# Pinning the issue order of operand splits and of pair sums, and merging the stores of hidden tiles, in a hybrid decoder step

## The chip, the cores and the metric

The kernel runs on one core of one Trainium2 chip. The metric is the device time of one execution in microseconds (us); before the change it is 2970.54 us, the median of three runs (2969.29 to 2973.55). The core has five engines that are named here as in the profile: PE (matmuls; PEld is its weight loads), DVE (vector engine), ACT (scalar engine), POOL (GpSimd) and SP, which does no arithmetic and issues all of this kernel's loads and stores.

## The reference

One layer of a decoder trunk on 1024 prompt tokens and 64 sample tokens, all in fp32. A first half-step SwiGLU feed-forward network, a token mixing with two branches (windowed pooling and a state-space scan), a second half-step SwiGLU network, and a final norm:

```python
def swiglu(x, w_in, w_out):
    gu = x @ w_in
    g, u = gu[..., :D_FF], gu[..., D_FF:]
    return (jax.nn.silu(g) * u) @ w_out
...
    x = x + 0.5 * swiglu(rmsnorm(x, norm_ffn1[l]), ffn1_w_in[l], ffn1_w_out[l])
    mix, new_pool, new_conv, new_ssm = token_mixing(
...
    x = x + mix
    x = x + 0.5 * swiglu(rmsnorm(x, norm_ffn2[l]), ffn2_w_in[l], ffn2_w_out[l])
```

D_MODEL is 1024 and D_FF is 2816, so the hidden layer has 22 blocks of 128 rows. The change touches the hand-over of the hidden layer `silu(g) * u` to the product with `w_out`, in both networks.

## The kernel before

**Numbers.** Each fp32 operand is split into a high part in the PE's 32-bit matmul format and the remainder; a product is then three matmuls (high with high, low with high, high with low). A split is two instructions: ACT copies the operand into the high part (`hh`, `hp`, `wh`), DVE subtracts that from the operand for the low part (`hr`, `hp`, `wl`). `split` (L357 for ACT, L359 for DVE) does it for tiles of activations, and `parts` (L759, L760) for weights. `parts` runs at high priority, `split` doesn't.

**Halves.** The 1088 tokens are worked in two halves of 512 and 576 tokens (h = 0, 1). FFN1's and FFN2's first matmul (`ffn_in`) runs over the 22 hidden blocks `ff` and, for each, over the halves. The result of one block and half is a tile `g`, whose two parts (slices `f` and `s_`, 256 or 288 columns each) are the two column halves of a Strassen-Winograd scheme.

**`hidden` and `hidden_odd`.** Two consecutive blocks `ff` make a pair: the even one is kept as `e`, the odd one arrives as `g`. The second matmul is done as seven products "1" to "7", each of which needs its own operand made of these four quarters: "1" is `e[f]`, "2" and "3" are `g[f]` and `g[s_]`, and "5", "6", "7" and "4" are results of four subtractions on POOL (L708), each in place over a quarter that is no longer needed. Every operand is stored to device memory into a tile `hb<product>_<pair>` (L691 for "1", L699 for the others) as soon as it exists: seven stores for each pair and half. The subtractions are a chain that starts `H_AT` = 0.3 us after `hidden_odd`, one step per `H_PACE` = 0.3 us, by the modelled PE time below.

**`second`.** The second matmul runs through the products in the order "1256473". A product has four units m (128 output columns each). A unit reads eleven X tiles (k = 0 to 10, one per pair) in three chunks of weights, kb = 0, 4 and 8, and runs 66 matmuls into two PSUM tiles `po`, one per half. `weights` gives a chunk: raw weights `wraw` are loaded (L748), for products 5, 6, 7 and 3 POOL adds or subtracts them (`ws`, L777 to L792), and `parts` makes `wh` and `wl` from it. `fetch_X` (L726 to L738) loads the X tiles of a product (`hr`, or `hp` where the tile is one of a ring of eight pairs) from `hb`; after each unit it issues up to three loads of the next product. `split_X` (L740 to L743) splits what has been loaded. It is called at the start of a product and, in `unit`, just before the chunk kb = 8. `leave` (L824) takes a finished `po` into the sums, and `old` (L794) adds old results that are loaded as `xo` (L798, L804).

**What sets the order.** The program is traced in the order in which the generators run. `tick` runs the chains (`start`, `later`) whose due time, counted in modelled PE time `pe[0]`, has come. A scheduler then orders the traced instructions on each engine by priority and by when its own model says that operands are ready, so an instruction can stand on its engine ahead of others that were traced before it. `keep_in_program_order` ties an instruction behind the one that was traced before it on the same engine. All engines work in order: what stands behind a waiting instruction waits too. SP issues loads and stores of all stages in one order.

**FFN1's loads.** While the first matmul of FFN1 runs, the second half's x is loaded in pieces `xin` (L965) and transposed on PE (`ptr`, helper L170; other matmuls come from the helper L166: `pu`, `pg` and `pw` are `ffn_in`'s PSUM tiles). Weight parts for later are stored and loaded in between (`part`, `pr`, L311 to L318).

Of the kernel before, what the change touches and what calls it, by code (L numbers as in the profile page):

```python
# [8 lines left out]
F32 = mybir.dt.float32  # L9
F32R = mybir.dt.float32r  # L10
I32 = mybir.dt.int32
AF = mybir.ActivationFunctionType
ALU = mybir.AluOpType

P = 128
# [27 lines left out]

N_FP = 4
NK2, N2, HALF_AT = NFF // 2, 544, (0, 256)
H_AT, H_PACE = 0.3, 0.3
AHEAD = {'2': 11, '5': 11, '6': 8, '4': 8, '7': 10, '3': 10}
STEP = (5.0, 3.8)
STEP_S = 1.0
# [15 lines left out]
def tile_hybrid_pool_ssd_macaron(  # L65
# [10 lines left out]
    V, S, T, G = nc.vector, nc.scalar, nc.tensor, nc.gpsimd  # L76
    dma = nc.sync.dma_start
# [3 lines left out]
    dp = ctx.enter_context(tc.tile_pool(name="dram", bufs=1, space=bass.MemoryType.DRAM))  # L81
# [7 lines left out]
    def act(shape=(P, 576), dt=F32, name="a"):  # L89
        return sp.tile(list(shape), dt, tag="act", bufs=N_ACT, name=nm(name))  # L90

    def pair(n, name="hl"):
        t = sp.tile([P, 2, 576], F32R, tag="pair", bufs=N_PAIR, name=nm(name))
        return t[:, 0, :n], t[:, 1, :n], t
# [16 lines left out]
    def fx(dt=F32, name="x"):  # L111
        if stage["name"] == "mix":
            return act((P, 576), dt, name)
        return stage["p"].tile([P, 592], dt, tag="fx", bufs=N_FX, name=nm(name))
# [22 lines left out]
    def start(gen, delay=0.0):  # L137
        c = Chain(gen, delay)
        chains.append(c)
        return c  # L140
# [214 lines left out]
    def split(src, hi, lo, scale=1.0):  # L355

        S.activation(hi, src, AF.Identity, scale=scale)  # L357
        if isinstance(scale, float) and scale == 1.0:
            V.tensor_tensor(lo, src, hi.bitcast(F32), op=ALU.subtract)  # L359
        else:  # L360
            V.scalar_tensor_tensor(lo, src, scale, hi.bitcast(F32), op0=ALU.mult, op1=ALU.subtract)
# [253 lines left out]
    def ffn_in_plain(wi, ff, x):  # L615

        h = x[0]
        g = fx(name="g")
        pg, pu = banks([x], "pd", "pg")[0], banks([x], "pd", "pu")[0]
        for kb in (0, 4):  # L620
            ws = [load_w(wi, kb, 4, c0 + ff * P) for c0 in (0, FF)]
            for kk in range(4):
                for pts, (wh, wl) in zip((pg, pu), ws):
                    products([pts], wh, wl, kk, slice(0, P), [x], kb + kk, KD)
                    tick()
        func(g, pg, h, AF.Silu)
        for pt, (a, b) in zip(pu, PIECES[h]):
            V.tensor_tensor(g[:, a:b], g[:, a:b], pt[:, : b - a], op=ALU.mult)
        hidden(h, ff, g)
# [46 lines left out]
        yield from gen  # L676


    hblock = {p: [dp.tile([P, N2], F32, tag=f"hb{p}_{i}", name=f"hb{p}_{i}") for i in range(NK2)] for p in "1234567"}
    even, hsums = [None, None], []  # L680

    def hidden(h, ff, g):

        if ff == NFF - 1:
            hlast.append(lambda: hidden_odd(h, ff, g))
        elif ff % 2:
            hidden_odd(h, ff, g)
        else:
            even[h] = g
            n, at = NPAIR[h], HALF_AT[h]  # L690
            dma(hblock["1"][ff // 2][:, at : at + n], g[:, :n])  # L691

    def hidden_odd(h, ff, g):

        n, i, at = NPAIR[h], ff // 2, HALF_AT[h]
        f, s_ = slice(0, n), slice(n, 2 * n)

        def put(p, x):
            dma(hblock[p][i][:, at : at + n], x)  # L699

        e = even[h]
        put("2", g[:, f])
        put("3", g[:, s_])

        def sums():
            for p, out, a, b in (("5", e[:, s_], e[:, s_], e[:, f]), ("6", g[:, s_], g[:, s_], e[:, s_]),
                                 ("7", e[:, f], g[:, s_], e[:, f]), ("4", g[:, f], g[:, f], g[:, s_])):
                G.tensor_tensor(out, a, b, op=ALU.subtract)  # L708
                put(p, out)
                yield H_PACE  # L710

        hsums.append(start(sums(), H_AT))

# [2 lines left out]
    def second(wo, after, half):  # L716
# [9 lines left out]
        def fetch_X(p, n):  # L726
            for k in range(len(X[p]), min(len(X[p]) + n, NK2)):
                if k >= 4:
                    a, r = act((P, 576), F32R, "hh"), act((P, 576), name="hr")
                elif p == "1":  # L730
                    a, r = fx(F32R, "hh"), fx(name="hr")
                else:
                    a, r, _ = pair(576, "hp")
                    r = r.bitcast(F32)
                a, r = a[:, :N2], r[:, :N2]
                dma(r, hblock[p][k])  # L736
                raws.append((k, r, a))
                X[p].append((a, r.bitcast(F32R)))  # L738

        def split_X(below=NK2):  # L740
            while raws and raws[0][0] < below:
                _, r, a = raws.pop(0)
                split(r, a, r.bitcast(F32R))  # L743

        def raw(par, mh, m, kb, nk):
            t = sp.tile([P, 4 * P], F32, tag="wraw", bufs=N_RAW, name=nm("wraw"))[:, : nk * P]
# [77 lines left out]
        def leave(p, m, h, pt):  # L824
# [30 lines left out]
            else:  # L855
                add(a[:, s_], a[:, s_])

        fetch_X("1", NK2)
        split_X()
        while hlast:  # L860
            hlast.pop(0)()
        while hsums:
            finish(hsums.pop(0))
        for p, nxt in zip(order[:-1], order[1:]):
            split_X(8)
            fetch_X(p, NK2)
            for m in range(4):
# [10 lines left out]
                n = AHEAD[nxt] - len(X[nxt])  # L878
# [1089 lines left out]
```

## Time and profile before

| | |
|---|---|
| median of three runs | 2970.54 us |
| profiled execution, its own time | 2973.63 us |
| its span, first to last instruction | 2971.9 us |
| PE busy | 2805.6 us (94%) |
| DVE, ACT, POOL busy | 62%, 47%, 46% |
| mean granted PE clock | 0.978 |
| DMA, of 16 engines' span | 54.9% |
| stores of hidden tiles | 308 issues |
| ACT splits of X tiles | 154 (106 `hh`, 48 `hp`) |

A row of the table of waits names the waiting engine, its PSUM or SBUF tile and line, then the releaser: the engine or transfer whose end came last before the wait ended. A row of a timeline gives the start in us from the span's start, the length, the engine and line, the operation with its tiles (out<-in, buffer numbers left out), how many in a row, and in square brackets the idle time before it and the releaser. The granted clock is the share of full speed that the PE was given; a matmul at half clock takes almost twice as long and counts as busy.

The stages that concern the change lie as follows: FFN1's first matmul up to 561 us, FFN1's `second` from 561 to about 840 us, FFN2's first matmul up to about 2686 us, FFN2's `second` from there to the end.

### The profile page before, as it was taken

What the parts mean: (1) busy time and instruction counts of PE and PEld (TensorE: products, weight loads), DVE (VectorE), ACT (ScalarE), POOL (GpSimd) and SP (SyncE); (2) the same over time, 40 slices, a digit from 0 to 9 for tenths busy, and PEclk for the clock granted to TensorE, in tenths of its full rate; (3) what the DMA queues carried; (4) which work ended last, traced back from release to release, by engine and by line L of the source; (5) the groups of instructions that cost most, each with busy time, mean ns of one, the idle gap of its engine ahead of it and who ended that gap; (6) DMA issues with size and microseconds to landing.
All of it is one profiled execution on the core that took longest, in us unless ns stands there. A gap on an engine that the chain in (4) does not pass through costs nothing. (4 is left out here: it accounts for less than half of the span.)

```text
span 2971.9 us, 54814 instructions
## 1 busy us (share of the span) xinstructions
PE 2805.6 (94%) x19834; PEld 2622.8 (88%) x19834; DVE 1852.5 (62%) x2848; ACT 1396.8 (47%) x3086; POOL 1354.8 (46%) x1424
## 2 busy tenths in 40 slices
PE   7989999989999999999999999898999999999888
PEld 6888899888979999999987887677999999989887
DVE  6645555656685486867676767866665554556665
ACT  5444444533354465555545656566233444444333
POOL 5645665344452264655632233323135656561651
PEclk9999999999999999999999999998999999999999
DMA  4566543576635555554367577786774333336772
GB/s 134 157 214 194 177 135 99 185 219 193 208 109 153 161 168 179 167 162 131 99 207 222 181 221 243 239 258 186 228 253 145 100 103 103 98 121 197 229 234 85
DMA packets 566864, 512.50 MB, mean 172 GB/s; under 512 B 39860, under 2 KB 435496, under 8 KB 566584
## 3 DMA queue, kind: packets, MB, share of 16 engines
q1 hardware_dynamic: 566576, 508.99, 54.9%
q8 instruction: 156, 2.56, 0.4%
q14 instruction: 116, 0.95, 0.1%
q10 hardware_dynamic: 16, 0.00, 0.0%
HBM read 361.28 MB, written 147.80 MB: 171 GB/s over the span
## 5 line engine op out<-in xcount | busy, mean ns | idle before, releaser
L166 PE MATMUL pw<-X,wh 128*128 128x288 f32 (+2 forms) x2832 | 634.6, 312 | 11.5 <-ACT v L566 9.8
L166 PEld LDWEIGHTS pw<-X,wh 128*128 128x128 f32 x2832 | 466.8, 191 | 35.7 <-ACT v L566 11.1
L166 PE MATMUL pw<-X,wl 128*128 128x288 f32 (+1 forms) x1644 | 476.8, 290 | 0.9 <-DVE wl L450 0.9
L450 DVE TENSOR_TENSOR wl<-s,wh 128x512 fp32r<-128x512 f32 x288 | 249.1, 866 | 285.4 <-ACT wh L449 263.9
L166 PE MATMUL pw<-hl,wh 128*128 128x256 f32 (+1 forms) x1536 | 392.0, 328 | 3.4 <-DVE t L570 3.3
L166 PE MATMUL pw<-hi,wh 128*128 128x288 f32 x1120 | 331.3, 296 | 2.4 <-ACT t L602 1.4
L166 PE MATMUL pw<-hi,wl 128*128 128x288 f32 x1120 | 330.0, 295 | 0.0
L166 PE MATMUL pw<-lo,wh 128*128 128x288 f32 x1120 | 329.7, 294 | 0.0
L443 POOL TENSOR_TENSOR s<-wraw,wraw 128x512 f32<-128x512 f32 x144 | 196.3, 1363 | 280.7 <-DVE wl L450 205.2
L166 PEld LDWEIGHTS pw<-X,wl 128*128 128x128 f32 x1644 | 315.1, 192 | 1.1 <-DVE wl L450 1.1
L166 PE MATMUL pw<-hl,wl 128*128 128x256 f32 x1072 | 300.3, 280 | 0.0
L166 PEld LDWEIGHTS pw<-hl,wh 128*128 128x128 f32 x1536 | 258.9, 189 | 24.5 <-DVE t L570 3.7
L449 ACT ACTIVATE wh<-s 128x512 fp32r<-128x512 f32 x288 | 181.0, 629 | 155.0 <-PE pw L166 129.7
L450 DVE TENSOR_TENSOR wl<-wraw,wh 128x512 fp32r<-128x512 f32 x216 | 177.5, 822 | 115.7 <-ACT wh L449 106.7
L166 PE MATMUL po<-hh,wh 128*128 128x256 f32 (+1 forms) x848 | 191.6, 298 | 31.6 <-ACT wh L759 31.5
L166 PEld LDWEIGHTS pw<-hi,wh 128*128 128x128 f32 x1120 | 210.5, 188 | 9.6 <-ACT t L602 2.0
L166 PEld LDWEIGHTS pw<-lo,wh 128*128 128x128 f32 x1120 | 210.6, 188 | 0.0
L166 PEld LDWEIGHTS pw<-hi,wl 128*128 128x128 f32 x1120 | 210.1, 188 | 0.2
L166 PEld LDWEIGHTS pw<-hl,wl 128*128 128x128 f32 x1072 | 203.0, 189 | 0.0
L449 ACT ACTIVATE wh<-wraw 128x512 fp32r<-128x512 f32 x216 | 135.5, 627 | 138.6 <-PE pw L166 117.3
L166 PE MATMUL po<-hh,wl 128*128 128x256 f32 (+1 forms) x848 | 191.0, 297 | 3.0 <-DVE wl L760 2.8
L166 PE MATMUL po<-hr,wh 128*128 128x256 f32 (+1 forms) x848 | 189.8, 295 | 1.0 <-DVE hr L359 1.0
(397 smaller groups left out, 6817.7 us busy)
## 6 DMA issues: line engine op xcount, KB each, us to landing
wraw<-in_ffn_w_in_dram SPq DMA_DIRECT2D x188, 256.0 KB
wraw<-in_ffn_w_out_dram SPq DMA_DIRECT2D x144, 256.0 KB
wraw<-in_w_in_dram SPq DMA_DIRECT2D x144, 256.0 KB
wh<-part SPq DMA_DIRECT2D x116, 256.0 KB
wl<-part SPq DMA_DIRECT2D x116, 256.0 KB
hr<-hb SPq DMA_DIRECT2D x106, 272.0 KB
hb<-g SPq DMA_DIRECT2D x154, 144.0 KB
hb<-g SPq DMA_DIRECT2D x154, 128.0 KB
```

The lines of the kernel that those rows point to most:

```text
L166: T.matmul(out, lhsT, rhs, start=start, stop=stop, skip_group_check=free)
L443: G.tensor_tensor(t, a, b, op=op)
L449: S.activation(wh, a, AF.Copy)
L450: V.tensor_tensor(wl, a, wh.bitcast(F32), op=ALU.subtract)
```

## The change

**Stores.** The seven tiles `hb` of a pair become four: "1" alone, and "23", "75" and "46" as tiles that hold two products side by side. "2" and "3" are stored in one transfer of both quarters of `g`. The four subtractions run without stores between them, 0.5 us apart, starting 3.0 us after `hidden_odd`; 3.0 us after the last, "75" (the tile `e`) and "46" (the tile `g`) are stored in one transfer each. So a pair and half has four stores in place of seven, of the same bytes. Loads remain one per product and pair.

**Order of the subtractions.** They and the two late stores are pinned to the traced order on their engines. For the first pair of each network (ff = 1) they run on DVE, otherwise on POOL.

**Splits of X tiles.** The ACT half of `split_X` is pinned to the traced order (and is the function Copy in place of Identity); the DVE half is not pinned.

On ACT, at the end of a unit of a product whose weights are sums (FFN1's `second`); `wh` are weight chunks, `hp` and `hh` the high parts of X tiles. Before:

```order
665 L759 ACTIVATE wh_8646<-ws_8640 128x512
666 L357 ACTIVATE hp_8748<-hp_8748 128x544
667 L357 ACTIVATE hp_8750<-hp_8750 128x544
668 L357 ACTIVATE hp_8752<-hp_8752 128x544
669 L759 ACTIVATE wh_8680<-ws_8674 128x512
670 L759 ACTIVATE wh_8714<-ws_8708 128x384
671 L357 ACTIVATE hp_8872<-hp_8872 128x544
672 L357 ACTIVATE hh_8874<-hr_8875 128x544
673 L357 ACTIVATE hh_8877<-hr_8878 128x544
```

The first chunk of a unit is followed by three splits of tiles of the next product, then the unit's other two chunks. Now:

```order
663 L767 ACTIVATE wh_8547<-ws_8541 128x512
664 L767 ACTIVATE wh_8581<-ws_8575 128x512
665 L767 ACTIVATE wh_8615<-ws_8609 128x384
666 L750 ACTIVATE hh_8527<-hr_8528 128x544
667 L750 ACTIVATE hh_8530<-hr_8531 128x544
668 L767 ACTIVATE wh_8669<-ws_8663 128x512
669 L767 ACTIVATE wh_8703<-ws_8697 128x512
670 L767 ACTIVATE wh_8737<-ws_8731 128x384
671 L750 ACTIVATE hp_8649<-hp_8649 128x544
672 L750 ACTIVATE hp_8651<-hp_8651 128x544
673 L750 ACTIVATE hp_8653<-hp_8653 128x544
```

The same three splits (`hp`, last three rows) stand behind the unit's third chunk (384 columns) and behind all three chunks of the unit after it; two splits of the product before stand where they stood.

On ACT, at the passage from FFN1's first matmul to `second`; L602 and L607 are `ffn_in`'s last evacuations, `wh<-wraw` chunks of product 1. Before:

```order
538 L602 COPY t_6268<-pw_1102_6315 128x288
539 L357 ACTIVATE hh_6386<-hr_6387 128x544
540 L357 ACTIVATE hh_6389<-hr_6390 128x544
541 L759 ACTIVATE wh_6465<-wraw_6463 128x512
542 L357 ACTIVATE hh_6392<-hr_6393 128x544
543 L357 ACTIVATE hh_6395<-hr_6396 128x544
544 L759 ACTIVATE wh_6495<-wraw_6493 128x512
545 L357 ACTIVATE hp_6554<-hp_6554 128x544
546 L607 ACTIVATE g_6269<-g_6269 128x288
547 L759 ACTIVATE wh_6525<-wraw_6523 128x384
548 L357 ACTIVATE hp_6651<-hp_6651 128x544
```

Seven `hh` splits of product 1 stand further up, between the weight chunks of the first matmul, and the last four of it here, among the first three chunks. Now (the row of L602 and the first two `hh` are the three rows ahead of these):

```order
532 L767 ACTIVATE wh_6366<-wraw_6364 128x512
533 L750 ACTIVATE hh_6299<-hr_6300 128x544
534 L750 ACTIVATE hh_6302<-hr_6303 128x544
535 L750 ACTIVATE hh_6305<-hr_6306 128x544
536 L750 ACTIVATE hh_6308<-hr_6309 128x544
537 L607 ACTIVATE g_6176<-g_6176 128x288
538 L750 ACTIVATE hh_6311<-hr_6312 128x544
539 L750 ACTIVATE hh_6314<-hr_6315 128x544
540 L750 ACTIVATE hh_6317<-hr_6318 128x544
541 L750 ACTIVATE hh_6320<-hr_6321 128x544
542 L750 ACTIVATE hh_6323<-hr_6324 128x544
543 L767 ACTIVATE wh_6396<-wraw_6394 128x512
```

All eleven splits of product 1 stand behind L602, five of them between L607 and the second chunk. On DVE the low parts follow them in the same way, seven `hr` between its last work for `ffn_in` (L609) and the `wl` of that second chunk.

On SP, in FFN1's first matmul; `hb` are the stores of hidden tiles, `xin` the pieces of x, `part` and `pr` prepared weights, `wraw` weights. Before:

```order
108 L699 DMA hb2_1_278<-g_259_1540 128x256
109 L469 DMA wraw_413_2369<-in_ffn1_w_in_dram 128x4x128
110 L699 DMA hb2_1_278<-g_264_1558 128x288
111 L699 DMA hb6_1_322<-g_259_1540 128x256
112 L699 DMA hb7_1_333<-g_146_866 128x256
113 L699 DMA hb6_1_322<-g_264_1558 128x288
114 L699 DMA hb4_1_300<-g_259_1540 128x256
115 L699 DMA hb7_1_333<-g_230_1373 128x288
116 L699 DMA hb4_1_300<-g_264_1558 128x288
117 L317 DMA part_317_1853<-ph_315_1850 128x512
118 L318 DMA part_319_1854<-pr_300_1768 128x512
119 L965 DMA xin2_323_1873<-in_x_prompt_dram 128x512
```

The load of `xin2_323` follows the stores of products "2", "6", "7" and "4" of a pair, each of the last three behind its subtraction. Now:

```order
98 L705 DMA hb23_1_278<-g_259_1499 256x1x256
99 L705 DMA hb23_1_278<-g_264_1519 256x1x288
100 L317 DMA part_317_1800<-ph_315_1797 128x512
101 L318 DMA part_319_1801<-pr_300_1728 128x512
102 L973 DMA xin2_323_1821<-in_x_prompt_dram 128x512
103 L311 DMA pr_329_1859<-in_ffn2_w_in_dram 128x4x128
104 L705 DMA hb75_1_289<-g_146_832 256x1x256
105 L705 DMA hb46_1_300<-g_259_1499 256x1x256
106 L973 DMA xin2_335_1914<-in_x_prompt_dram 128x512
```

That load stands behind the "23" stores alone; of the pair's late stores the first two come after it.

```diff
@@ -43,7 +43,7 @@
 
 N_FP = 4
 NK2, N2, HALF_AT = NFF // 2, 544, (0, 256)
-H_AT, H_PACE = 0.3, 0.3
+H_AT, H_PACE, H_OUT = 3.0, 0.5, 3.0
 AHEAD = {'2': 11, '5': 11, '6': 8, '4': 8, '7': 10, '3': 10}
 STEP = (5.0, 3.8)
 STEP_S = 1.0
@@ -676,7 +676,13 @@
         yield from gen
 
 
-    hblock = {p: [dp.tile([P, N2], F32, tag=f"hb{p}_{i}", name=f"hb{p}_{i}") for i in range(NK2)] for p in "1234567"}
+    hblock = {}
+    for ps_ in ("1", "23", "75", "46"):
+        for i in range(NK2):
+            t = dp.tile([P, len(ps_), N2], F32, tag=f"hb{ps_}_{i}", name=f"hb{ps_}_{i}")
+            hblock[ps_, i] = t
+            for j, p in enumerate(ps_):
+                hblock[p, i] = t[:, j, :]
     even, hsums = [None, None], []
 
     def hidden(h, ff, g):
@@ -688,26 +694,27 @@
         else:
             even[h] = g
             n, at = NPAIR[h], HALF_AT[h]
-            dma(hblock["1"][ff // 2][:, at : at + n], g[:, :n])
+            dma(hblock["1", ff // 2][:, at : at + n], g[:, :n])
 
     def hidden_odd(h, ff, g):
 
         n, i, at = NPAIR[h], ff // 2, HALF_AT[h]
         f, s_ = slice(0, n), slice(n, 2 * n)
 
-        def put(p, x):
-            dma(hblock[p][i][:, at : at + n], x)
+        def put(ps_, x):
+            return dma(hblock[ps_, i][:, :, at : at + n], x[:, : 2 * n].rearrange("p (a t) -> p a t", a=2))
 
         e = even[h]
-        put("2", g[:, f])
-        put("3", g[:, s_])
+        put("23", g)
 
         def sums():
-            for p, out, a, b in (("5", e[:, s_], e[:, s_], e[:, f]), ("6", g[:, s_], g[:, s_], e[:, s_]),
-                                 ("7", e[:, f], g[:, s_], e[:, f]), ("4", g[:, f], g[:, f], g[:, s_])):
-                G.tensor_tensor(out, a, b, op=ALU.subtract)
-                put(p, out)
+            for out, a, b in ((e[:, s_], e[:, s_], e[:, f]), (g[:, s_], g[:, s_], e[:, s_]),
+                              (e[:, f], g[:, s_], e[:, f]), (g[:, f], g[:, f], g[:, s_])):
+                tc.keep_in_program_order((V if ff == 1 else G).tensor_tensor(out, a, b, op=ALU.subtract))
                 yield H_PACE
+            yield H_OUT
+            for ps_, x in (("75", e), ("46", g)):
+                tc.keep_in_program_order(put(ps_, x))
 
         hsums.append(start(sums(), H_AT))
 
@@ -733,14 +740,15 @@
                     a, r, _ = pair(576, "hp")
                     r = r.bitcast(F32)
                 a, r = a[:, :N2], r[:, :N2]
-                dma(r, hblock[p][k])
+                dma(r, hblock[p, k])
                 raws.append((k, r, a))
                 X[p].append((a, r.bitcast(F32R)))
 
         def split_X(below=NK2):
             while raws and raws[0][0] < below:
                 _, r, a = raws.pop(0)
-                split(r, a, r.bitcast(F32R))
+                tc.keep_in_program_order(S.activation(a, r, AF.Copy))
+                V.tensor_tensor(r.bitcast(F32R), r, a.bitcast(F32), op=ALU.subtract)
 
         def raw(par, mh, m, kb, nk):
             t = sp.tile([P, 4 * P], F32, tag="wraw", bufs=N_RAW, name=nm("wraw"))[:, : nk * P]
```

## The prediction, made before the changed kernel was run

> **What bounds the kernel now.** I read the page first, then PE's busy time by stage, then what PE waited for, then the engine named there, then single stalls in order of time.
>
> ```profile
> span 2971.9 us, 54814 instructions
> PE 2805.6 (94%) x19834; PEld 2622.8 (88%) x19834; DVE 1852.5 (62%) x2848; ACT 1396.8 (47%) x3086; POOL 1354.8 (46%) x1424
> ```
>
> PE is the bound: 166.3 us of the span are all that earlier issue can recover, besides time at a low clock. The table by stretch says where that lies. Its columns are the stretch and its length, busy time of PE, PEld, DVE, ACT and POOL (with instruction counts), granted clock, DMA share, GB/s.
>
> ```profile
> 70.00:130.00 60.00, 52.83 (x360) 50.35 (x359) 39.12 (x53) 23.31 (x55) 36.82 (x33) 0.94 0.46 140
> 130.00:300.00 170.00, 156.21 (x1007) 145.97 (x1006) 88.56 (x156) 73.04 (x171) 84.42 (x85) 0.94 0.64 205
> 560.00:640.00 80.00, 74.41 (x571) 72.66 (x571) 42.56 (x68) 34.18 (x66) 13.00 (x11) 0.98 0.67 201
> 640.00:760.00 120.00, 103.66 (x786) 101.63 (x786) 71.21 (x98) 37.70 (x66) 67.65 (x54) 0.96 0.73 213
> 760.00:780.00 20.00, 19.42 (x133) 19.10 (x133) 17.86 (x24) 8.61 (x15) 17.87 (x15) 0.83 1.11 321
> 2690.00:2880.00 190.00, 172.39 (x1317) 169.62 (x1316) 108.05 (x153) 65.86 (x119) 76.75 (x61) 0.96 0.71 213
> 2880.00:2900.00 20.00, 17.98 (x126) 17.66 (x127) 18.19 (x25) 8.16 (x15) 16.68 (x14) 0.83 1.10 313
> ```
>
> 70 to 300 us is FFN1's first matmul (idle 7.2 and 13.8 us). 560 to 780 and 2690 to 2900 us are the two passes of `second` (idle 22.5 and 19.6 us). All of them show clocks under 1. What ended PE's idle time, over the whole span (total, times, longest):
>
> ```profile
> PE po L166 <- ACT wh L759: 33.8, 11, 7.2
> PE ptr L170 <- DMA xin<-in_x_sample_dram: 8.1, 2, 4.4
> PE po L166 <- DVE wl L760: 6.9, 9, 1.3
> PE ptr L170 <- DMA xin<-in_x_prompt_dram: 5.7, 2, 5.2
> PE pu L166 <- ACT wh L296: 4.9, 1, 4.9
> ```
>
> `po` belongs to `second`, `ptr` and `pu` to FFN1. ACT, which releases `po`, was itself waiting; first two rows 555 to 835 us, last two 2680 to 2972 us:
>
> ```profile
> ACT hp L357 <- DMA hp<-hb: 39.8, 12, 8.7
> ACT hh L357 <- DMA hr<-hb: 39.4, 16, 6.6
> ACT hp L357 <- DMA hp<-hb: 39.7, 13, 8.3
> ACT hh L357 <- DMA hr<-hb: 33.9, 17, 5.1
> ```
>
> One stall in order of time (start, length, engine, line, count):
>
> ```profile
> 749.58 1.29 POOL L786 TENSOR_TENSOR ws<-wraw,wraw 128x512 f32<-128x512 f32 x1 [1.62 <-DMA wraw<-in_ffn_w_out_dram]
> 751.87 1.44 SPq L736 DMA_DIRECT2D hp<-hb  x3
> 752.62 0.41 PE L166 MATMUL po<-hp,wh 128*128 128x256 f32 x2
> 752.87 0.41 PE L166 MATMUL po<-hp,wl 128*128 128x256 f32 x2
> 756.58 2.16 ACT L357 ACTIVATE hp<-hp 128x544 fp32r<-128x544 f32 x3 [7.96 <-DMA hp<-hb]
> 758.65 1.03 ACT L759 ACTIVATE wh<-ws 128x512 fp32r<-128x512 f32 x2
> 759.32 0.82 PE L166 MATMUL po<-hh,wh 128*128 128x256 f32 x2 [6.04 <-ACT wh L759]
> ```
>
> The sum `ws` was ready at 750.9. Its cast `wh` (758.65) stood on ACT behind three splits of X tiles whose loads were issued only at 751.87. PE had nothing left from 753.3 and started 0.67 us after that cast. The X tiles split there are read in the next product, after this cast's matmuls; their splits had been let ahead of a cast that was urgent.
>
> **The change, part by part.**
>
> *Splits pinned behind the casts traced before them.* The order now has a unit's three casts, then two or three splits. Counted in the orders on SP and PE, the next cast behind a split is first read 73 to 110 matmuls after the point at which that split's load can be issued at the old stall sites, and at least 127 now, mostly 180 to 480 for `hp`. At 0.125 us a matmul (the two PE rows of two above start 0.25 us apart) 73 are 9.1 us, which the ACT waits of up to 8.7 us plus the splits (0.7 us each) use up; 127 are 15.9 us, which they don't. So I take the `wh` waits as gone: −33.8 us. The `wl` waits stay (6.9): the DVE half isn't pinned.
>
> Stalls cost twice, since a low clock follows. After the shortest of the longer ones:
>
> ```profile
> 2705.53 0.70 PE L166 MATMUL po<-hh,wh 128*128 128x256 f32 x2 [2.35 <-ACT wh L759]
> 2708.35 0.66 PE L166 MATMUL po<-hh,wh 128*128 128x256 f32 x2
> ```
>
> Six pairs of matmuls lie between these starts, without idle time: 2.82 / 6 = 0.47 us a pair where 0.25 is usual. The shortfall of the clock in the table, (1 − clock) × length, is 1.6 + 4.8 + 3.4 = 9.8 us in the first pass and 7.6 + 3.4 = 11.0 in the second; part of it lies inside the idle time, so I take 8 each: −16. The Trainium skill (TensorE: Matmul & The Clock Gate, Part 1) says that the clock halves after an idle window of about 3.4 us. The trace disagrees for this stall: 2.35 us of idle were enough. By the page such a stall would cost no dip; with three of them below its figure, at some 1.3 us each (2.82 − 6 × 0.25), the term would be −12 by an estimate.
>
> *New block at the start of each pass.* All eleven splits of product 1 now stand behind FFN-in's last ACT work, five of them and seven DVE halves between L607/L609 and the second cast.
>
> ```profile
> 556.14 0.38 ACT L602 COPY t<-pw 128x288 f32<-128x288 f32 x1
> 560.90 0.41 PE L166 MATMUL po<-hh,wh 128*128 128x256 f32 x2
> 562.89 0.44 DVE L609 TENSOR_TENSOR g<-g,pw 128x288 f32<-128x288 f32 x1
> L357 ACT ACTIVATE hh<-hr x11: 642/649/667, 544.1 to 561.0; 128x544 fp32r<-128x544 f32 x11
> L359 DVE TENSOR_TENSOR hr<-hr,hh x11: 711/915/1291, 546.0 to 563.3; 128x544 fp32r<-128x544 f32 x11
> ```
>
> Before, the eleven were done from 544 on, beside FFN-in's matmuls. Now ACT starts them at 556.5. DVE's L609 may end up to one split (0.65) earlier than at 563.3, since no split stands ahead of the activation it reads; from 562.7, seven halves at 0.65 to 1.2 us (rows overlap by some 0.07) and one `wl` of 0.7 end between 568.0 and 571.8. The order puts the matmul that reads this `wl` 32 matmuls into the pass, 564.9 by 560.90 + 32 × 0.125. The stall is 3.1 to 6.9 us; by the median (0.915) 4.4, and a clock dip of 2 to 3 us follows. I take +7 for each pass (ends 2 and 10): +14.
>
> *FFN1: sums without stores between, three stores instead of six.*
>
> ```profile
> 145.28 7.41 SPq L699 DMA_DIRECT2D hb<-g  x7
> 153.71 0.45 SPq L965 DMA_DIRECT2D xin<-in_x_prompt_dram  x1
> 157.95 1.11 PE L170 MATMUL ptr<-ident,xin 128*128 128x128 f32 x4 [5.20 <-DMA xin<-in_x_prompt_dram]
>   DMA hb<-g: 38.4, 27
> ```
>
> SP spent 7.4 us on seven stores that waited, one by one, for GpSimd's sums (the last row: GpSimd idle before those sums until a store had landed); the load of `xin` behind them came 5.2 us late. In the new order this load stands ahead of the pair's "75" and "46" stores, and so do those behind the two later stalls (the 8.1 us row). −13.8 us of waits; of the clock's 0.06 × 170 = 10.2 us I take −8. A later `xin` moves the other way, from 85 matmuls of lead to 54, behind four stores: +4 (ends 0 and 6). Net −17.8.
>
> *First pair's sums on VectorE.*
>
> ```profile
> 73.70 1.55 POOL L708 TENSOR_TENSOR g<-g,g 128x256 f32<-128x256 f32 x2 [7.89 <-DVE g L628]
> 85.51 0.85 PE L166 MATMUL pu<-hi,wh 128*128 128x288 f32 x2 [4.93 <-ACT wh L296]
> ```
>
> GpSimd stood 7.89 us with the X chain of the second half queued behind a sum; that chain then held ACT, whose cast released PE at 85.51. Freed of it, some 6 of the stage's 7.2 us of idle go (4.9 here and part of the rest, which follows it), and 2.5 of the clock's 0.06 × 60 = 3.6. Against this, DVE's second sum must wait for the "23" store to land with a weight split behind it: +1.5 to 5, I take 3.5. Net −5. The 16 sums themselves, half as wide as an `hr` split (0.7 to 1.3), are under 1 us each on an engine busy for 39 of 60 us there.
>
> *Nothing.* Bytes are unchanged. Copy in place of Identity changes 154 splits of 0.65 us on an engine that is busy 47%; even 0.1 us more each would be hidden by its idle time, and without that idle time cost 15. 132 issues fewer on SP cost nothing where SP isn't waited for; the later stores of "75" and "46" are read two products on. From 300 to 540 and in FFN2's first matmul PE is full, so there is no gain there.
>
> Sum: −33.8 − 16 + 14 − 17.8 − 5 = −58.6 us. The profiled execution took 2973.6 (span 2971.9 plus 1.7), 3.1 above the median of 2970.5; 2970.5 − 58.6 = 2912.
>
> **Rivals.**
>
> *A: the transfers are the limit behind the splits.* Product 7 needs per unit two sets of raw weights, a quarter of eleven X tiles and a tile of `xo`:
>
> ```profile
> wraw<-in_ffn_w_out_dram SPq DMA_DIRECT2D x144, 256.0 KB
> hp<-hb SPq DMA_DIRECT2D x48, 272.0 KB
> ```
>
> 2 × (256 + 256 + 192) + 748 + 272 KB = 2.49 MB in 66 × 0.125 = 8.25 us, or 301 GB/s. The table shows 321 and 313 once each, for it, but 213 over 120 and 190 us, against. At 213 a unit takes 11.7 us: +3.4 × 4 × 2 = +27, 2939. The Trainium skill (DMA: Bandwidth & Descriptors, Specifications) gives about 358 GB/s of HBM per core, by which this rival costs nothing.
>
> *B: slower. The pinned splits become the wait.* A split that waits for its load now always holds the next unit's casts and the drains of PSUM on ACT. Now 40.7 us of PE idle (33.8 + 6.9) stand against 152.8 us of ACT waits for X loads (the four rows), 27%. If a share s came through, the change would be (152.8 s − 40.7) × 1.39 (the dips, 16 on 40.7) + 14 − 22.8. That is zero at s = 0.31 and +41 (3011) at 0.5. For it: nothing else may pass a waiting split. Against: the leads counted above.
>
> *C: the block at the start is hidden*, since loads or L609 come earlier: −58.6 − 14, 2898.
>
> *D: FFN1 gains nothing*, because the loads there are held by another store, and passes gain little beyond the block: within 6 us of 2970.
>
> **How the numbers follow.** Forecast 0.53, A 0.2, B 0.12, C 0.1, D 0.05. 0.2% is 6 us, about what a measurement can tell from no change. Faster: forecast, A and C, 0.83; the same 0.05; slower 0.12. The range reaches from C with the wider ends of the FFN1 terms (2885) past A to 2958, where A meets a block of 10 us in each pass and a smaller clock gain; it leaves out B and D.
>
> **What would show it.** Right: no `wh` stall over 2 us in either pass, granted clock 0.98 or more from 600 to 760, the waits of ACT for `hp` still there but no longer PE's; a stall of 3 to 7 us within 40 matmuls of a pass's first; no `ptr` stall at the second to fourth `xin`. Wrong: `po` waits on `wh` behind a split in most units (B), POOL's sums or `wraw` as releasers with DMA near 1 over product 7 (A), or a new wait of SP for a sum ahead of `xin` (D).

## The result, and the profile after

The changed kernel takes 2935.06 us (median of four, 2933.76 to 2937.11), the kernel before 2972.05 us in the same comparison: a ratio of 0.9866 (95% interval 0.9833 to 0.9900). By the medians it is faster by 37 us (1.2%), where 58.6 were forecast (the medians alone give 0.9876; the four runs of the kernel before include one of 2986.93 us). The profiled execution took 2934.26 us.

The page of the kernel after, its span and engines:

```profile
span 2932.5 us, 54478 instructions
PE 2793.1 (95%) x19834; PEld 2614.3 (89%) x19834; DVE 1876.5 (64%) x2864; ACT 1399.6 (48%) x3086; POOL 1349.2 (46%) x1408
```

The same matmuls run on PE in nearly the same order in both kernels, so their start times can be compared one by one. The table takes the same matmul (by its number on PE) in the two profiled executions. The last column is the forecast for that stretch.

| matmul, at us before | what lies there | after minus before, us | since the row above | forecast |
|---|---|---|---|---|
| 40.0 | ahead of anything the change touches | +3.2 | +3.2 | 0 |
| 103.2 | first pair's sums done | −0.2 | −3.4 | −5 |
| 551.8 | end of FFN1's first matmul | −17.3 | −17.1 | −17.8 |
| 572.3 | 11 us into the first pass of `second` | −8.9 | +8.4 | +7 |
| 802.6 | end of that pass | −28.7 | −19.8 | −24.9 |
| 2668.6 | end of FFN2's first matmul | −31.4 | −2.7 | 0 |
| 2694.1 | 8 us into the second pass | −21.4 | +10.0 | +7 |
| 2958.3 | last matmul | −39.0 | −17.6 | −24.9 |

(At the first of these matmuls the traces of all versions stand between −0.2 and +3.2 us, although the change touches nothing ahead of it; this part isn't the change's.)

PE's busy time by stretch, after (columns as before):

```profile
70.00:130.00 60.00, 54.45 (x368) 51.51 (x367) 43.78 (x69) 23.77 (x57) 25.45 (x23) 0.97 0.50 149
130.00:300.00 170.00, 164.36 (x1104) 153.05 (x1104) 101.04 (x164) 77.55 (x184) 100.54 (x97) 1.00 0.70 222
540.00:560.00 20.00, 12.16 (x74) 11.26 (x73) 15.55 (x18) 9.02 (x17) 10.07 (x9) 0.83 0.66 217
560.00:640.00 80.00, 80.00 (x642) 80.00 (x641) 45.63 (x68) 35.14 (x66) 14.68 (x11) 1.00 0.66 192
640.00:720.00 80.00, 78.43 (x628) 78.21 (x626) 64.25 (x80) 29.65 (x51) 54.45 (x43) 1.00 0.79 235
720.00:760.00 40.00, 33.31 (x231) 32.21 (x232) 27.11 (x36) 15.48 (x27) 27.57 (x25) 0.91 0.96 286
2670.00:2830.00 160.00, 160.00 (x1273) 159.96 (x1272) 108.50 (x146) 64.59 (x117) 68.39 (x52) 0.99 0.72 213
2830.00:2862.00 32.00, 25.95 (x162) 24.40 (x161) 18.70 (x27) 10.98 (x19) 21.23 (x19) 0.84 0.93 276
```

PE is full from 560 to 640 and from 2670 to 2830 us, at a clock of 0.99 to 1. The loss has gathered at two places in each pass: the start (540 to 560) and product 7 (720 to 760, 2830 to 2862). At product 7 the DMA engines are busy 93 to 96%. PE's waits over the whole span:

```profile
PE po L166 <- ACT wh L767: 16.2, 10, 3.3
PE po L166 <- DVE wl L768: 10.5, 6, 4.9
PE pw L166 <- DVE wl L450: 6.0, 2, 5.1
PE pu L166 <- DVE wl L297: 5.3, 4, 2.5
PE ptr L170 <- DMA xin<-in_x_prompt_dram: 4.3, 4, 1.8
```

Before, the `wh` row had 33.8 and the two `xin` rows 13.8. What ACT waited for in the passes (first two rows 545 to 790 us, last two 2655 to 2930):

```profile
ACT wh L767 <- POOL ws L794: 23.1, 12, 5.2
ACT hh L750 <- DMA hr<-hb: 19.0, 9, 6.4
ACT wh L767 <- POOL ws L794: 21.8, 12, 4.6
ACT hh L750 <- DMA hr<-hb: 18.4, 10, 6.0
```

The waits for `hp`, 39.8 and 39.7 before, are no longer among the largest, and those for `hr` have halved. In their place casts wait for GpSimd's sums of product 7. The start of the first pass, where all splits of product 1 stand as a block, on ACT, DVE and PE:

```profile
545.31 2.83 ACT L750 ACTIVATE hh<-hr 128x544 fp32r<-128x544 f32 x5
548.04 1.54 ACT L767 ACTIVATE wh<-wraw 128x512 fp32r<-128x512 f32 x3
545.58 8.43 DVE L751 TENSOR_TENSOR hr<-hr,hh 128x544 fp32r<-128x544 f32 x7
555.27 0.82 PE L166 MATMUL po<-hh,wl 128*128 128x256 f32 x2 [4.86 <-DVE wl L768]
```

The seven low parts take 1.2 us each, the `wl` that PE wants stands behind them, and PE idles 4.86 us (3.58 in the second pass, where the seven took 7.88 us). And the first chunk of product 7's first unit, on SP, POOL and PE:

```profile
712.54 1.45 SPq L743 DMA_DIRECT2D hr<-hb  x3
714.30 7.64 SPq L756 DMA_DIRECT2D wraw<-in_ffn_w_out_dram  x6
719.42 2.83 POOL L794 TENSOR_TENSOR ws<-wraw,wraw 128x512 f32<-128x512 f32 x2 [3.46 <-DMA wraw<-in_ffn_w_out_dram]
721.73 0.78 PE L166 MATMUL po<-hp,wh 128*128 128x256 f32 x4 [3.30 <-ACT wh L767]
```

The raw load was issued at 714.30, behind three X tiles and at the moment when a sum of GpSimd's ended (714.27) and freed a slot; it landed by 719.3. The sum, the cast and PE follow one another at once.

### The profile page after: what moved, and what is told of

Its sections match the earlier page's. It is cut to its first block, busy times and chain, and to the rows that moved or that the text cites. A ratio compares the mean times of both kernels' runs of the same rounds, so it can differ in the third digit from the quotient of the medians.

```text
span 2932.5 us, 54478 instructions
## 1 busy us (share of the span) xinstructions
PE 2793.1 (95%) x19834; PEld 2614.3 (89%) x19834; DVE 1876.5 (64%) x2864; ACT 1399.6 (48%) x3086; POOL 1349.2 (46%) x1408
## 3 DMA queue, kind: packets, MB, share of 16 engines
q8 instruction: 156, 2.56, 0.4%
## 5 line engine op out<-in xcount | busy, mean ns | idle before, releaser
L166 PE MATMUL pw<-X,wh 128*128 128x288 f32 (+2 forms) x2832 | 625.9, 310 | 3.8 <-ACT v L566 3.5
L450 DVE TENSOR_TENSOR wl<-s,wh 128x512 fp32r<-128x512 f32 x288 | 234.0, 813 | 257.1 <-ACT wh L449 233.3
L450 DVE TENSOR_TENSOR wl<-wraw,wh 128x512 fp32r<-128x512 f32 x216 | 189.4, 877 | 139.7 <-ACT wh L449 131.5
```

Of the source, the lines that this page charges most:

```text
L166: T.matmul(out, lhsT, rhs, start=start, stop=stop, skip_group_check=free)
L450: V.tensor_tensor(wl, a, wh.bitcast(F32), op=ALU.subtract)
```

## The experiments

Each ratio below is to the kernel before in the same comparison, with its 95% interval; a difference to the changed kernel is one between the medians of two comparisons. A trace is a single execution, and executions of one kernel differ by several us (2966.14 to 2985.24 in the ten of the kernel with the delays alone), so traces are compared stage by stage. "At 572" and the like are the times of the table above, by the same matmul against the kernel before.

**The two halves of the change apart.** The splits alone, on the kernel before:

```diff
-                split(r, a, r.bitcast(F32R))
+                tc.keep_in_program_order(S.activation(a, r, AF.Copy))
+                V.tensor_tensor(r.bitcast(F32R), r, a.bitcast(F32), op=ALU.subtract)
```

> The kernel before with one part of the change: the ACT half of the splits of X tiles pinned (as Copy), stores, sums and delays as before. Theory (the parts add up, read from the two traces matmul by matmul): the passes of second lose the stalls behind late splits, -19 and -17 us, and get the block at their start, +8 and +8; FFN1's first matmul stays as before. Sum -20: 2952 us against 2972. Rival 1 (the stores, too, make the passes faster, since fewer issues stand ahead of X loads on SP): the passes gain less than 10 net, 2960 or more. Rival 2 (nearly all of the gain is in the splits): 2940 or less.

Measured: 2946.84 us against 2975.96, ratio 0.9909 (0.9892 to 0.9926). By its profile it stands at +0.8 us at 552, +6.2 at 572, −12.9 at 803, −14.1 at 2669, −5.3 at 2694 and −22.9 at the end. FFN1's first matmul gained nothing; both passes show the stalls removed and the block added. 29 us by the medians lie between the theory and rival 2; 23 us by the traces are the theory's 20 nearly.

The rest alone: the changed kernel with the diff above reversed, that is, with `split` again and nothing pinned there.

> The changed kernel without the pin on the splits: stores merged, sums pinned and later, first pair on VectorE. Theory (the parts add up): FFN1's loads of x on time, -17 us up to the first pass, the early stretch even, both passes with the stalls behind late splits as before, and no block at their start. 2972 - 17 = 2955 us. Rival (the X loads in the passes also come earlier by the merged stores): the wh stalls in the passes shrink too, 2945 or less.

Measured: 2950.04 us, ratio 0.9919 (0.9899 to 0.9939), between theory and rival. In its profile −16.3 at 552, −18.4 at 572, −20.8 at 803, −19.6 at 2669, −19.4 at the end. PE's waits in `second`:

```profile
PE po L166 <- ACT wh L766: 29.3, 9, 7.6
PE ptr L170 <- DMA xin<-in_x_prompt_dram: 3.8, 4, 1.9
```

The `wh` stalls remain (29.3 us, before 33.8) and the long `xin` stalls are gone, as the theory said. In the traces the parts add up: −22.9 − 19.4 = −42.3 against −39.0 together, in which the +3.2 of the opening are held. The medians don't show it: 29 + 26 = 55 us for the parts against 37 together, by the ratios 0.91% + 0.81% against 1.34%, a difference within the intervals.

**Order or time of the stores?** The kernel before, with the two delays and nothing else of the change:

```diff
-H_AT, H_PACE = 0.3, 0.3
+H_AT, H_PACE = 3.0, 0.5
```

> The kernel before with the two delays alone (sums start 3.0 us after the pair and follow each other by 0.5 us); six stores per pair and half, each between sums, nothing pinned. Theory (the stores gated one by one by GpSimd hold SP, the order matters, not the time): little changes, the stalls before xin stay at 2 us or more each, 2965 to 2975 us. Rival (the later start alone lets the loads of x go ahead): the xin stalls go, about -15 us, 2958 or less.

Measured: 2973.53 us, ratio 1.0005 (0.9991 to 1.0019): nothing. All three `xin` stalls are there; the first on PE:

```profile
162.06 1.12 PE L170 MATMUL ptr<-ident,xin 128*128 128x128 f32 x4 [5.07 <-DMA xin<-in_x_prompt_dram]
```

Starting the sums later doesn't bring the loads of x forward by itself. It takes the rest: the stores merged, put behind all four sums and pinned. Which of those three matters, and whether they need the delays, wasn't tried apart.

**Where the first pair's sums run.** All on GpSimd:

```diff
-                tc.keep_in_program_order((V if ff == 1 else G).tensor_tensor(out, a, b, op=ALU.subtract))
+                tc.keep_in_program_order(G.tensor_tensor(out, a, b, op=ALU.subtract))
```

> The changed kernel with the first pair's sums on GpSimd like all others (still pinned). Theory: VectorE no longer waits for the landing of the 23 store, so the 5.1 us stall in FFN2's first matmul and the 2 to 2.5 us ones near 72 and 81 us go; GpSimd's X chain near 75 to 90 us gets the sums back but they come 3 us later and wait for no store between, so about half of the old 4.9 us stall returns. About 2935 - 4 = 2931 us (2927 to 2935). Rival (VectorE was the better place, the chain on GpSimd is what holds ACT): the early stretch loses 6 to 9 us, 2938 or more.

Measured: 2934.44 us, ratio 0.9876 (0.9852 to 0.9900), no different from the changed kernel in sum, but not for want of effects. In its profile FFN1's early stretch loses (a stall of 4.01 us at 87.00 and one of 2.11 at 90.43; +2.2 from 40 to 103 us in place of −3.4, and −10.8 at 552 in place of −17.3), as the rival said. FFN2's stall of 5.07 us is gone, as the theory said, but one of 4.04 us that waits for ACT's `v` (L566) stands in that stage; the kernel before had one of that kind, 3.1 us. In the changed kernel the 5.07 us were, on DVE and PE:

```profile
2245.85 1.40 DVE L713 TENSOR_TENSOR g<-g,g 128x288 f32<-128x288 f32 x1 [5.69 <-DMA hb<-g]
2248.97 0.53 PE L166 MATMUL pw<-hi,wl 128*128 128x288 f32 x1 [5.07 <-DVE wl L450]
```

DVE waited 5.69 us for the "23" store to land, with a `wl` behind it. And the block at the start of the passes became cheaper, with the same order of instructions. The block and GpSimd beside it, all sums on GpSimd:

```profile
551.54 4.53 DVE L751 TENSOR_TENSOR hr<-hr,hh 128x544 fp32r<-128x544 f32 x7
551.97 6.43 POOL L610 TENSOR_TENSOR g<-g,t 128x288 f32<-128x288 f32 x1 [12.03 <-DMA hp<-hb]
```

and in the changed kernel, GpSimd beside the 8.43 us of the block shown above:

```profile
545.48 0.81 POOL L610 TENSOR_TENSOR g<-g,t 128x288 f32<-128x288 f32 x1 [12.04 <-ACT g L607]
546.24 1.23 POOL L713 TENSOR_TENSOR g<-g 128x256 f32<-128x256 f32 x1
547.55 2.27 POOL L713 TENSOR_TENSOR g<-g,g 128x256 f32<-128x256 f32 x2
```

Either the seven DVE instructions take 8.43 us and GpSimd's go on beside them, or they take 4.53 us and one GpSimd instruction that takes 0.81 us elsewhere takes 6.43. The second passes repeat it (7.88 us; 4.54 and 6.57). This is what two engines would show that share something and hold each other off. The Trainium skill (GPSIMD Engine Reference, Specifications) says that GpSimd's access to on-chip memory is shared with VectorE and contended by DVE instructions with two operands there; these subtractions are of that kind, and the rows agree. Why DVE came through in one run and not in the other isn't settled.

**The last pair's sums left out.** The direct test of that contention:

```diff
-                tc.keep_in_program_order((V if ff == 1 else G).tensor_tensor(out, a, b, op=ALU.subtract))
+                if ff < NFF - 1:
+                    tc.keep_in_program_order((V if ff == 1 else G).tensor_tensor(out, a, b, op=ALU.subtract))
```

> The changed kernel without the four subtractions of the last pair (left out: eight per network, so three products of that pair get wrong operands; its stores stay). They run on GpSimd beside the block of seven VectorE splits at the start of each pass, which took 8.43 us there, and 4.53 us in the first pass of the run with all sums on GpSimd, where GpSimd's instruction beside it took 6.43 us. Theory (the two engines hold each other up on these instructions, so the block costs twice what it must): the seven splits take 4.5 to 5 us in both passes, the 4.9 and 3.6 us stalls shrink to 1.5 or less, 4 us each with the clock: 2935 - 8 = 2927 us. Rival (the splits are slow from their transfers or their operands' place): they take 8 us or more still, 2933 to 2937.

Measured: 2918.95 us, ratio 0.9823 (0.9806 to 0.9841), 16 us less than the changed kernel (13 by the ratios), more than the 8 expected. DVE at the start of the first pass:

```profile
546.63 2.60 DVE L752 TENSOR_TENSOR hr<-hr,hh 128x544 fp32r<-128x544 f32 x3
549.16 0.68 DVE L769 TENSOR_TENSOR wl<-wraw,wh 128x512 fp32r<-128x512 f32 x1
549.76 2.62 DVE L752 TENSOR_TENSOR hr<-hr,hh 128x544 fp32r<-128x544 f32 x4
```

Alone, the last four halves take 0.66 us each, as expected. But the scheduler also put the `wl` in among the seven, which nothing pins on DVE, so PE had it some 5 us earlier. The run shows that the block's price can go to nothing (+0.7 from 552 to 572 us in place of +8.4), not how much of that is the contention. The run with all sums on GpSimd, whose DVE kept its order, tells more: +3.0 there, and +3.2 in place of +10.0 at the second start, so where DVE came through, each pass lost 5 to 7 us less at its start.

**The block unpinned.** The changed kernel with the pin taken off product 1's splits:

```diff
-        split_X()
+        split_X(pin=False)
```

where `pin=False` leaves out `keep_in_program_order`.

> The changed kernel with the pin taken off the splits of product 1 alone, the ones that now stand as a block at the start of each pass. Theory: the stalls of 6 to 7 us within the first 40 matmuls of each pass and the low clock after them go, 8 us each: 2935 - 16 = 2919 us, with no po stall over 1.5 us in the first 10 us of a pass. Rival (the time is given back: what is early then waits for weights or sums in the later products): 2928 or more.

Measured: 2920.69 us, ratio 0.9819 (0.9801 to 0.9837), 14 us less than the changed kernel. In its profile the first pass begins without a stall over 1.5 us and stands at −18.0 at 572 (−8.9 in the changed kernel), the second at −38.6 at 2694 (−21.4); little is given back (−57.5 at the end, −39.0 in the changed kernel; 3.4 of this difference lie in the opening). From 552 to 572 it gains 2.3 us where the changed kernel loses 8.4, from 2669 to 2694 it gains 1.3 where that loses 10.0: the block cost 11 us in each pass by the traces; by the medians the two kernels differ by 14 in all. PE's waits:

```profile
PE po L166 <- ACT wh L769: 11.3, 6, 3.3
PE po L166 <- DVE wl L770: 4.0, 5, 0.9
```

**What limits product 7?** One of its two raw weight tiles is left out:

```diff
-                    x, y = raw(0, 0, m, kb, nk), raw(0, 1, m, kb, nk)
+                    x = y = raw(0, 0, m, kb, nk)
                     with tc.high_priority(hp[0]):
-                        G.tensor_tensor(a, x, y, op=ALU.subtract)
+                        G.tensor_tensor(a, x, y, op=ALU.add)
```

> The changed kernel in which product 7 loads one of its two raw weight tiles per chunk and adds it to itself (left out: the other half of that product's weights, so its part of the result is another). GpSimd's sums, their number and their buffers stay. Theory (the waits in product 7 for the sum ws are waits for transfers): the stalls of 1.3 to 3.3 us before ws in product 7 of both passes (721 to 748 and 2833 to 2859 us) and the low clock after them go, 9 and 8 us: 2935 - 16 = 2919 us. Rival (GpSimd is too slow for sums and additions of xo together, transfers are hidden): the same stalls stay, 2932 to 2936.

Measured: 2930.58 us (2922.07 to 2936.62), ratio 0.9844 (0.9821 to 0.9867); by the time, between theory and rival. The trace tells more. The stalls in which a cast waited for `ws` are gone in both passes, with the number of GpSimd's sums as it was, so they were waits for transfers, or for the six slots (`N_RAW`) into which raw weights are loaded. The run doesn't part the two, since half the loads also need half the slots. In the changed kernel both are seen around the first pass's stalls (waits of SP from 705 to 760 us):

```profile
705.00:718.00 13.00, 13.00 (x106) 13.00 (x105) 4.27 (x7) 2.84 (x5) 5.04 (x4) 1.00 0.67 197
730.00:742.00 12.00, 9.90 (x77) 9.46 (x76) 7.36 (x10) 3.43 (x6) 8.64 (x9) 1.00 1.14 320
SPq L756 <- POOL ws L794: 6.9, 4, 3.5
SPq L756 <- POOL ws L800: 4.5, 4, 1.7
```

Ahead of the 3.30 us stall the DMA engines had room (0.67), while raw loads stood on SP until GpSimd's sums had freed a slot; from 730 to 742 their share was 1.14. The stalls come from both, late issue and full engines, and their shares aren't shown.

What the run gained is another matter. The first pass got little of it: in place of −24.8 from 572 to 770 us it has −31.3, and then, from 770 to 803 us, +11.6 in place of +5.1. On ACT and PE, at the start of product 3:

```profile
767.14 0.66 ACT L750 ACTIVATE hh<-hr 128x544 fp32r<-128x544 f32 x1 [6.28 <-DMA hr<-hb]
769.30 0.61 ACT L767 ACTIVATE wh<-ws 128x512 fp32r<-128x512 f32 x1
769.97 0.58 PE L166 MATMUL po<-hh,wh 128*128 128x256 f32 x1 [6.74 <-ACT wh L767]
```

This is the stall of the kernel before in its old form: a split waits for the last X tiles, whose load could be issued only at 764.1, and holds a cast that PE wants. In the changed kernel product 7's stalls gave those tiles time. In the second pass a stall of 3.1 us at product 7's first casts is of the same form: three splits waited 8.1 us for X tiles, with the sum long ready. So the same kernel with the last splits of product 3 behind the casts:

```diff
         fetch_X("3", NK2)
-        split_X()
...
-                if kb == 8 and len(hs) == 2:
+                if kb == 8 and (len(hs) == 2 or p == "3"):
                     split_X()
```

> The run with one raw load in product 7, in which the last two splits before product 3 are traced, and so pinned, behind the third weight chunk of product 3's first unit instead of ahead of its second. Theory (without the ws stalls, the pass reaches product 3 earlier than its last X tiles do, and the pinned splits of these hold the casts): the 6.7 us stall at 770 us and its counterpart of 3.1 us at 2840 go, 9 and 5 us with the clock: about 2930 - 12 = 2918 us. Rival (the first unit of product 3 waits for the X tiles themselves or for sums): 2926 or more.

Measured: 2928.5 us, ratio 0.9854 (0.9829 to 0.9879), runs from 2920.37 to 2936.14; the times don't tell it from the run before. In the trace the 6.74 us stall is gone, and 2.91 us are left, released by a split of an X tile itself. The one at 2840 us, which is at product 7 and not, as the expectation had it, a counterpart at product 3, fell to 1.1. The mechanism at product 3 is the theory's; its price is under what these runs can tell.

**What the real kernel can do about it.** Three versions on top of the unpinned block. First, half of product 7's additions of old results moved into product 3, which loads no weights:

```diff
                 elif p == "7":
                     old(m, 1, 0)
-                    old(m, 0, 1)
...
             for m in range(4):
+                if h == 0:
+                    old(m, 0, 1)
+                    late_.pop(0)()
                 unit("3", m, [h], kept[m] if h else keep(m))
```

> The kernel with product 1 unpinned, and one of product 7's two loads and additions of xo per unit moved into product 3, which loads no weights. Theory (product 7 has too much to move and to add): its ws stalls shrink by half or more, 4 to 8 us over both passes, and product 3 hides the moved work: 2920.7 - 6 = 2915 us. Rival (what holds ws are its own raw loads, which wait for slots; xo doesn't matter, or the late additions hold the end of a pass): 2920 or more.

Measured: 2924.74 us, ratio 0.9834 (0.9819 to 0.9848): the rival. The first `ws` stall of the first pass fell from 3.25 to 1.83 us, but stalls of 2.56, 1.09 and 2.07 us came at 738 to 762 us, and a `ws` stall of 5.80 us in the second pass, where there had been 1.61.

Second, the first pair's sums on DVE in FFN1 alone (`passes` is a list that `second` appends to):

```diff
-                tc.keep_in_program_order((V if ff == 1 else G).tensor_tensor(out, a, b, op=ALU.subtract))
+                tc.keep_in_program_order((V if ff == 1 and not passes else G).tensor_tensor(out, a, b, op=ALU.subtract))
```

> The kernel with product 1 unpinned, and the first pair's sums on VectorE only in FFN1, on GpSimd in FFN2. Theory: the 3.5 to 5.1 us stall in FFN2's first matmul, where VectorE waits for the 23 store to land with a weight split behind it, goes: 2920.7 - 4 = 2917 us. Rival (the time comes back within that stage, which is bound by something else): 2920 to 2922.

Measured: 2912.59 us, ratio 0.9802 (0.9779 to 0.9826), the lowest median of all, some 59 us under the kernel before and 22 under the changed one. The stall (3.5 us in the unpinned version) is gone; in its place the one of the kernel before that waits for ACT's `v` is back, with 2.76 us. In the traces this version gains 2.2 us on the unpinned one over that stage (2258 to 2321 us), and only that stage is touched. The medians are 8 us apart, the ratios 5, and the two intervals overlap, so more than the 2 us isn't shown.

Third, on that version, at most two X tiles of products 7 and 3 loaded after each unit before:

```diff
-                fetch_X(nxt, min(n, 3))
+                fetch_X(nxt, min(n, 2 if nxt in "73" else 3))
```

> The run with product 1 unpinned and FFN2's first pair on GpSimd, in which at most two, not three, X tiles of products 7 and 3 are loaded after each unit before. Theory (X loads just ahead of raw weights delay product 7's sums): its first ws stall (1.9 and 2.5 us) shrinks to under 1 us, but three X tiles are left for the start of products 7 and 3, so 2912.6 - 2 = 2911 us (2908 to 2914). Rival (the X tiles left for the start hold these products): 2918 or more.

Measured: 2917.68 us, ratio 0.9818 (0.9801 to 0.9834). The trace shows the rival's mechanism: stalls of 6.02 and 5.70 us stand at product 7's first unit: ACT waited 7.58 us for the first of its late X tiles, with the cast that PE wanted behind their splits. Most of it was made up for within the passes (the first is 3 us longer than in the version without this, the second 1 us shorter), and the intervals overlap, so a price isn't shown. And the splits of product 3 behind the casts, on the fastest version:

> The run with product 1 unpinned and FFN2's first pair on GpSimd, in which the last two splits before product 3 stand behind the third chunk of its first unit. No stall stood there in that run, since the ws stalls of product 7 gave the X tiles time. Theory: the same within the measurement, 2909 to 2914 us. Rival (the casts of product 3 come earlier and the small waits there go): 2908 or less.

Measured: 2916.57 us (2912.02 to 2923.56), ratio 0.9821 (0.9800 to 0.9842), above what theory and rival had. The intervals overlap: no different from the version without it as far as these runs can tell.

## Why the prediction was right in direction and too high

- **What bounded the kernel: right.** Splits of late X tiles ahead of urgent casts were the stalls; pinning them alone takes them away, and leaving them unpinned alone keeps them.
- **"I take the `wh` waits as gone: −33.8 us": too much.** 16.2 us of them are left, some 12 in product 7 behind the sum `ws` and 3.5 at the starts of the passes. In the traces the passes gave −37.4 us beyond their start (−19.8 − 17.6), where −49.8 with the clock were forecast. This is the term that failed, by 12 us. Product 7 gained nothing: from the end of product 4 to the first matmul of product 3 it took 43.3 and 43.6 us before and takes 45.8 and 45.2 now, where its 264 matmuls at 0.125 us are 33.0. Its two stalls behind splits (6.0 and 7.2 us) went, and waits for its sums took their place.
- **Rival A** named that cause, the loads of product 7, and so is half of what came: the measured 2935 lie 4 us from its 2939 and 23 from the forecast's 2912. It was priced as a whole other case at +27; it belonged into the sum, since the table already had the DMA share at 1.1 there. Product 7 is now 25 us above full pace in the two passes, near the 27, but that is luck in part: A took 213 GB/s, where the rate there was 286, and it counted one tile of `xo` per unit where the code loads two: 2.76 MB in 8.25 us, or 335 GB/s, more than any stretch of its table reached (321). It also had no term for the wait for slots. By the page of the Trainium skill cited there (DMA: Bandwidth & Descriptors, Specifications, about 358 GB/s) A would have cost nothing. No stretch shown here reached that rate: 286 GB/s stand beside a DMA share of 0.96 over 40 us, 320 beside 1.14 over 12.
- **The signs that it had set** came out on both sides. As said, a stall of 3 to 7 us stands within 40 matmuls of each pass's first (4.86 and 3.58 us), and the waits for `hp` aren't PE's any more. But `wh` stalls over 2 us are left in both passes (3.30; 2.89, 2.46 and 2.16), the clock is 0.91 from 720 to 760 us, and POOL's sums as releasers with a DMA share near 1 are the sign of A.
- **The clock after stalls: right in kind.** Where stalls went, the clock rose from 0.96 to 1.00, and around the new ones it is 0.83 to 0.91.
- **The block at the start, +14: right, measured +18.4** by the table. The step "seven halves at 0.65 to 1.2 us" came out at its upper end, 1.2; where DVE came through, with all sums on GpSimd, it was 0.65, so the contention with GpSimd makes the difference.
- **FFN1's loads of x, −17.8: −17.1.** The delays alone did nothing; with the merged and pinned stores the gain came.
- **First pair on VectorE, −5: −3.4.** The wait for the "23" store with a weight split behind it, foreseen for FFN1 at 1.5 to 5 us, is 5.07 us in FFN2, where no gain stands against it; the prediction had FFN2's first matmul at nothing. Moving it there to GpSimd is worth 2 us in the traces; a stall of the kernel before comes back with it.
- **Rival B** didn't come at the strength that decides, but its mechanism is real: it appeared at product 3 as soon as product 7 was made faster (6.74 us), and with fewer X tiles ahead (6.02 us).

## What to carry to other kernels

On an in-order engine, the urgent instruction must not be placed behind one that waits for a load: ask of each pinned or floating split what stands behind it, and by how many matmuls its load's issue leads. When such a stall goes, look for the resource that the stall had been giving time to: here the transfers of one product, then the last operand tiles of the next. Pin what must not run ahead, and leave free what fills gaps: the pin that took the stalls out of both passes cost 11 us at the start of each, by the traces.

## What the runs showed of the hardware beyond that

DVE's subtractions and GpSimd's arithmetic on fp32 tiles in on-chip memory held each other up strongly in these runs, and not evenly: the same seven DVE instructions took 8.43 us or 4.53 us, and the same GpSimd instruction 0.81 us or 6.43 us. A store of 288 KB was seen to take 6.9 us from its issue to its landing (a "23" store, 2238.9 to 2245.8 in the changed kernel), and DVE stood idle for the last 5.69 of them. And a load's end isn't a matter of its own length: raw weights of 256 KB landed 3.1 us after their issue at one place (702.5 us in the changed kernel) and 5.0 us after it behind three X tiles (714.3).
